# Holding back the odd mixer's first weight splits, and moving the even mixer's first scores by one and two products

## The chip, the cores and the metric

The kernel runs on one core of a Trainium2 chip. The metric is the device time of one execution in microseconds. The engines are TensorE (PE: matmuls, and PEld: its weight loads), VectorE (DVE), ScalarE (ACT), GpSimd (POOL) and SyncE (SP, which here only issues transfers). Each engine works through its own queue in order.

## The reference, cut to what matters

A trunk of two layers over 256 tokens of width 1024, in float32:

```
for layer in (0, 1):
    x = x + 0.5 * swiglu(rms_norm(x), gate, up, down)     # 2816 hidden columns
    x = x + mixer(rms_norm(x))                            # even mixer in layer 0, odd mixer in layer 1
    x = x + 0.5 * swiglu(rms_norm(x), gate, up, down)
return rms_norm(x)
```

The even mixer has two groups of eight heads: "a" is global attention with normed queries and keys and a 2-D rotary, "b" is windowed attention with a 1-D rotary and a sink. The odd mixer is neighbourhood attention with a learned bias table, 16 heads. Each mixer ends with an output projection.

## The kernel before

The stages are numbered 0 to 5: SwiGLU (0), even mixer (1), SwiGLU (2), SwiGLU (3), odd mixer (4), SwiGLU (5). The tokens are two tiles of 128 (`tt` is 0 or 1).

**Products and splits.** Each float32 product is made of three matmuls of rounded parts: high by high, high by low, low by high. `mm` issues these three (lines L471 to L473) and then calls `tick`. Weights come by DMA into tiles called `raw` (three of them, plus a smaller kind). They are then split: ScalarE copies the high part (`hi`, L479), VectorE subtracts to get the low part (`lo`, L482). A split of the mixers is "narrow": it is made in two halves of 128x512, each called a split below, and each half serves one product per token tile. The SwiGLUs' weights are split in double width, 128x1024. The tiles for finished parts are limited: `FIT["wp"]` is 7, each holding two halves, and one is free again when both of its halves were used by both token tiles. When the last split of a `raw` tile is made, the next `raw` transfer is issued on SP's queue.

**The order of the work.** Nothing is planned on the chip: the order in each engine's queue is the order in which the Python code issues the instructions, and that is set by `tick`. Each product makes one tick. In a tick first the pending low part is issued, then every task that is due takes a step (a task is a generator that yields the number of ticks until its next step), and then the supply of splits is advanced:

```
            self.due += self.rate
            n = self.whole[0].step() if self.whole else 1
            if self.due >= n and self.room():
                self.due = min(self.due - n, n)
                self.supply()
```

So `rate` is the number of splits per product. If a product's split has not been made when the product is issued, `mm` makes it at once. Where code must wait for a task's result (`ready`, `finish`, the loop in `out_proj`), it calls `tick(False)`: tasks step, but no product is issued and no split is supplied.

**The end of a SwiGLU.** The down projection runs over 11 pairs of hidden blocks in the order of `DOWN`; some are done by Strassen's seven products (`seven`), whose accumulators "1", "5", "6" and "7" are added to x by the task `combine` (a step per product, eight steps) when the last Strassen pair is through. Then `ENDS` sets the rate and sets `due` to 0. The last two pairs (`HELD`) follow as 16 products, ordered by token tile and half of the columns, so that after each four products `add_to_x` (L614) can add one quarter of x. Five ticks after that, `prepare` transposes the quarter on TensorE (L527) for the next stage.

**The odd mixer.** Two groups of eight heads; for each, keys, queries and values are projected in turn: six projections of 16 products, each using eight new splits in the first eight products (token tile 0) and the same eight again (token tile 1). `natural` turns keys and queries over on TensorE (L549), and ScalarE and VectorE split them (`okTz`, `okTx`, `oqT`). `ODD_RATE` has the rate of each projection and of the two parts of the output projection. The attention runs as a task beside the products.

**The even mixer.** One projection for the keys and values of both groups, then queries of "b", queries of "a", and the output projection for "b" and for "a", 16 products each. `queries` waits `ROPE_WAIT` ticks for VectorE's rotary before the transposes of the queries of "b" (L549). `attend` starts one pair of heads after the other, `EVEN_GAP` ticks apart; each pair issues scores (L1055, L1056, L1059), maxima, exponentials (L1095), normalising (GpSimd, L1109), transposes (L1117) and products with the values (L1040). Group "b" is done before group "a" begins. The output projection of "a" needs its results `oTa00h` and so on, and waits for them with `tick(False)`.

Of the kernel before, what the change touches and what calls it, by code (L numbers as in the profile page):

```python
# [57 lines left out]
SUMS_WAIT = [8, 2]  # L58
SILU_WAIT = [3, 4, 2]
NAT_WAIT = 2  # L60
ROPE_WAIT = [3, 3]
KB_WAIT = {
    "a": [8, 7],
    "b": [8, 9],
# [68 lines left out]
class Split:  # L133
# [3 lines left out]
    def __init__(self, raw, uses, last=False, narrow=False, kind="wp", then=None):  # L137
        self.raw, self.last, self.narrow, self.kind, self.then = raw, last, narrow, kind, then
        n = raw.shape[1]
        self.left = sum(uses[i % len(uses)] for i in range(n))  # L140
        self.parts, self.made = None, 0
# [64 lines left out]
class Trunk:  # L206
# [4 lines left out]
    def __init__(self, ctx, tc, a, out):  # L211
        self.ctx, self.tc, self.nc, self.a, self.out = ctx, tc, tc.nc, a, out
        pool = lambda name, bufs, **kw: ctx.enter_context(tc.tile_pool(name=name, bufs=bufs, **kw))
        self.one = pool("one", 1)
        self.ph = None
        self.raw = pool("raw", RAWS)
        self.wp = pool("wp", FIT["wp"])

        self.two = pool("two", 2)
        self.acc = pool("acc", 1, space=PSUM)  # L220
        self.n = 0
        self.rate = RATE[0]
        self.tasks, self.last, self.last_v = [], [], [[], []]
        self.units, self.whole, self.queue, self.due, self.half = self.plan(), [], [], 0, None
        self.live = {kind: 0 for kind in FIT}
        self.ahead = len(FIRST) - RAWS

        self.hts = {}

    def name(self, s):  # L230
# [56 lines left out]
    def room(self):  # L287

        if not self.whole:
            return False  # L290
        split = self.whole[0]
        return split.made > 0 or self.live[split.kind] < FIT[split.kind]


# [364 lines left out]
    def ffn(self):  # L659
# [197 lines left out]
        for ci, w in enumerate(FF_CHUNKS):  # L857
# [11 lines left out]
            for tt in range(NT):  # L869
                g = both[tt] if self.now.n + ci == 0 else self.project(self.ready(tt), G, tags[tt])  # L870
# [9 lines left out]
        for tt in range(NT):  # L880
            both = self.project(self.now.hT[tt], V, "s")
            s = self.t([P, 512], "silu", SILUS[self.now.n])
# [25 lines left out]
        def seven(pair, first, last):  # L908
            b11, b21, b22, t7, t5, t8, t6 = self.take(7)
            if first:  # L910
                for task in tasks:
                    self.finish(task)
                self.rate = DOWN_RATE[self.now.n]
            f = 2 * pair
            while f not in sums:
                self.tick(False)

            def temp(name, tag, lh, piece):
                if first:
                    M[name] = self.bank(tag)  # L920
                self.mm(M[name], lh, piece, first, last)

            d3, d1, d2, d4 = sums[f]
            temp("1", "pj", gT[0][f + 1], b11)
            self.mm(Y[0][0], gT[0][f], b21, False, False)
            self.mm(Y[0][1], d4, b22, False, False)
            temp("7", "tp", d3, t7)
            temp("5", "s", d1, t5)
            self.mm(Y[1][0], gT[1][f], t8, False, False)
            temp("6", "tp", d2, t6)  # L930

        def combine():

            op = nc.vector.scalar_tensor_tensor
            x = lambda tt, i: self.x[tt][:, i * 512 : i * 512 + 512]
            more = lambda o, y: nc.vector.tensor_tensor(o, o, y, op=ALU.add)
            c = self.t([P, 512], "silu", SILUS[self.now.n])
            nc.scalar.activation(c, M["1"], AF.Copy, scale=0.5)
            op(x(0, 0), M["1"], 0.5, x(0, 0), op0=ALU.mult, op1=ALU.add)
            yield 1  # L940
            v = self.t([P, 512], "silu", SILUS[self.now.n])
            op(v, M["6"], 0.5, c, op0=ALU.mult, op1=ALU.add)
            yield 1
            w = self.t([P, 512], "glu", 3)
            op(w, M["7"], -0.5, v, op0=ALU.mult, op1=ALU.add)
            yield 1
            y = self.t([P, 512], "silu", SILUS[self.now.n])
            op(y, M["5"], 0.5, v, op0=ALU.mult, op1=ALU.subtract)
            yield 1
            more(x(0, 1), y)  # L950
            z = self.t([P, 512], "glu", 3)
            yield 1
            op(z, M["5"], 0.5, w, op0=ALU.mult, op1=ALU.subtract)
            yield 1
            more(x(1, 0), w)
            yield 1
            more(x(1, 1), z)

        order = [i for i, (kind, _) in enumerate(down) if kind == "strassen"]
        for i, (kind, pair) in enumerate(down[:-HELD]):  # L960
            if kind == "strassen":
                seven(pair, i == order[0], i == order[-1])
                if i == order[-1]:
                    self.start(combine())
                    self.rate, self.due = ENDS[self.now.n]
                continue
            for f in (2 * pair, 2 * pair + 1):
                W[f] = self.take(2)
                for tt in range(NT):
                    for half in range(2):  # L970
                        use(f, tt, slice(half * 512, half * 512 + 512))
# [12 lines left out]
                self.start(self.add_to_x(tt, sl, Y[tt][sl.start // 512] if to is None else to, 0.5))  # L984


    def attend(self, qT, has_q, kT, v, has_v, tag, dest, gap, waits, norm, sink=None, bias=None, scale=None):

        nc = self.nc
        pT, sums, exs = {}, {}, {}

        def pair(tt, b0, s):
            wait = iter(waits[tt * 4 + b0 + s])
            if s == 0:
                sums[tt, b0] = self.little([P, 2, 2], "sums", 4)
                exs[tt, b0] = None if sink is None else self.little([P, 2, 2], "es", 4)
            e = exs[tt, b0]
            S = self.scores(tt, b0, s, qT(tt), kT, sink is not None)  # L1000
            yield next(wait)
            src, m, by = self.maxima(S, tt, b0, s, sink, bias, scale)
            if e is not None:
                nc.gpsimd.tensor_tensor(e[:, s, :], sink[:, s * 4 + b0 : s * 4 + b0 + 2], m, op=ALU.add)
            yield next(wait)
            p = self.exps(src, m, by, sums[tt, b0][:, s, :])
            if e is not None:
                nc.scalar.activation(e[:, s, :], e[:, s, :], AF.Exp)
            self.normalise(p, sums[tt, b0][:, s, :], None if e is None else e[:, s, :], norm)
            yield next(wait)  # L1010
            tb = self.transposed(p)
            yield next(wait)
            pT[tt, b0, s] = self.t([P, 2, 2, P], "pt", 4)
            flat = pT[tt, b0, s].rearrange("p a b c -> p (a b c)")
            nc.scalar.activation(flat, tb, AF.Copy)
            if s == 0:
                return
            yield next(wait)
            O = self.bank("o")[:, : 2 * P]
            while not has_v():  # L1020
                yield 1
            self.weigh(O, b0, v, pT[tt, b0, 0], pT[tt, b0, 1])
            yield next(wait)
            yield from self.split_psum(O, 2, f"{tag}{tt}{b0}", dest[tt])

        for tt in range(NT):
            for b0 in (0, 2):
                for s in range(2):
                    while not has_q(tt, b0):
                        yield 1  # L1030
                    self.start(pair(tt, b0, s))
                    yield gap[tt * 4 + b0 + s]
        while len(dest[NT - 1]) < 4:
            yield 1
# [125 lines left out]
    def even(self, sink):  # L1160
# [8 lines left out]
        kT = {g: self.keys_tiles([P, T], f"kT{g}") for g in "ab"}  # L1169
        vv = {g: [self.t([P, P], f"v{g}{tt}") for tt in range(NT)] for g in "ab"}  # L1170
        qT = {g: [[], []] for g in "ab"}
# [26 lines left out]
        def queries(g, tt, ps):  # L1198
# [12 lines left out]
            else:  # L1211
                self.rope(nc.vector, qr, x, 8, axial[g], *tab[g][tt][:2], r)
                yield ROPE_WAIT[tt]
            tb = self.turned(qr.rearrange("p j s d -> p (j s d)"))
# [3 lines left out]
        def heads(g):  # L1218
            return self.attend(
                lambda tt: qT[g][tt],  # L1220
                lambda tt, b0: len(made[g]) > 2 + tt and all(task[1] is None for task in made[g][: 3 + tt]),
                lambda b: kT[g],
                lambda b, s, kc: vv[g][kc][:, s * HD : s * HD + HD],
                lambda: True,
                f"oT{g}",
                oT[g],
                EVEN_GAP[g],
                EVEN_WAITS[g],
                nc.gpsimd,
                sink=sink if g == "b" else None,  # L1230
                scale=(lambda tt, b, s: by[tt][:, s * 4 + b : s * 4 + b + 2]) if g == "a" else None,
            )
# [333 lines left out]
```

## Time and profile before

| what | value |
|---|---|
| median of 3 runs | 942.59 us (941.84 to 943.52) |
| the profiled execution | 942.41 us, span 940.6 us |
| TensorE busy | 921.9 us (98%) |
| VectorE busy | 782.9 us (83%) |
| ScalarE busy | 677.8 us (72%) |
| GpSimd busy | 92.5 us (10%) |

The span is the time from the first to the last instruction of the program; the rest of the execution's time lies around it. A row of the timeline has the start in us, the duration in us, the engine, the line of the kernel, the operation, output and inputs by the kernel's names, the shape, and the count of like instructions merged into the row. A bracket at the end gives how long the engine sat idle before the row, and what released it. Several matmuls overlap in TensorE's pipeline, so the time from one start to the next is what a matmul costs there, not its duration.

### The profile page before, as it was taken

What the parts mean: (1) busy time and instruction counts of PE and PEld (TensorE: products, weight loads), DVE (VectorE), ACT (ScalarE), POOL (GpSimd) and SP (SyncE); (2) the same over time, 40 slices, a digit from 0 to 9 for tenths busy, and PEclk for the clock granted to TensorE, in tenths of its full rate; (3) what the DMA queues carried; (4) which work ended last, traced back from release to release, by engine and by line L of the source; (5) the groups of instructions that cost most, each with busy time, mean ns of one, the idle gap of its engine ahead of it and who ended that gap; (6) DMA issues with size and microseconds to landing.
All of it is one profiled execution on the core that took longest, in us unless ns stands there. A gap on an engine that the chain in (4) does not pass through costs nothing.

```text
span 940.6 us, 12391 instructions
## 1 busy us (share of the span) xinstructions
PE 921.9 (98%) x4399; PEld 752.7 (80%) x4399; DVE 782.9 (83%) x1212; ACT 677.8 (72%) x1091; POOL 92.5 (10%) x152
## 2 busy tenths in 40 slices
PE   9999999999999999999999999999999999999997
PEld 6887888877878788888888878778878788878886
DVE  6799778778869989888978897999767687986997
ACT  7678975477787778875657778657877577768753
POOL 1300000064410000000100000008030000000001
PEclk9999999999999999999999999999999999999999
DMA  8857875554326577766467777565534458487761
GB/s 297 282 166 247 250 234 194 182 152 106 101 91 201 205 231 233 236 212 250 152 179 228 194 239 224 210 244 172 164 106 136 134 178 247 139 253 217 230 224 45
DMA packets 129343, 183.16 MB, mean 195 GB/s; under 512 B 50688, under 2 KB 63744, under 8 KB 129280
## 3 DMA queue, kind: packets, MB, share of 16 engines
q1 hardware_dynamic: 128704, 181.58, 60.9%
q8 instruction: 34, 0.56, 0.2%
q10 hardware_dynamic: 576, 0.79, 0.2%
q14 instruction: 29, 0.24, 0.1%
HBM read 169.76 MB, written 1.05 MB: 182 GB/s over the span
## 4 chain that ended last, share of the span: by engine, by line
PE 66%; DVE 16%; ACT 10%; DMA 4%; issue 3%; POOL 0%; SPq 0%; POOLq 0%; ACTq 0%; DVEq 0%
PE pj L471 9%; PE pj L472 9%; PE pj L473 9%; PE s L472 9%; PE s L473 9%; PE s L471 9%; DVE lo L482 7%; ACT hi L479 3%; DMA glu<-turned 2%; ACT turned L560 2%; DVE raw L395 2%; PE o L1040 2%; ACT shi L479 2%; PE tp L1117 1%; PE o L473 1%
## 5 line engine op out<-in xcount | busy, mean ns | idle before, releaser
L482 DVE TENSOR_TENSOR lo<-raw,hi 128x1024 fp32r<-128x1024 f32 (+1 forms) x372 | 375.9, 1030 | 80.8 <-ACT hi L479 79.3
L479 ACT ACTIVATE hi<-raw 128x1024 fp32r<-128x1024 f32 (+1 forms) x372 | 318.4, 889 | 49.9 <-PE pj L473 12.2
L471 PE MATMUL pj<-hi,th 128*128 128x512 f32 x367 | 146.7, 400 | 0.9 <-ACT glu L766 0.9
L472 PE MATMUL s<-lo,th 128*128 128x512 f32 x373 | 145.5, 390 | 0.9 <-DVE lo L482 0.7
L471 PE MATMUL s<-hi,th 128*128 128x512 f32 x373 | 146.2, 392 | 0.0
L472 PE MATMUL pj<-lo,th 128*128 128x512 f32 x367 | 143.9, 392 | 2.3 <-DVE lo L482 2.0
L473 PE MATMUL s<-hi,tl 128*128 128x512 f32 x373 | 145.3, 390 | 0.0
L473 PE MATMUL pj<-hi,tl 128*128 128x512 f32 x367 | 143.3, 390 | 0.0
L472 PEld LDWEIGHTS pj<-lo,th 128*128 128x128 f32 x367 | 69.1, 188 | 17.6 <-DVE lo L482 5.1
L472 PEld LDWEIGHTS s<-lo,th 128*128 128x128 f32 x373 | 70.0, 188 | 16.2 <-DVE lo L482 2.0
L473 PEld LDWEIGHTS s<-hi,tl 128*128 128x128 f32 x373 | 70.0, 188 | 14.6
L471 PEld LDWEIGHTS s<-hi,th 128*128 128x128 f32 x373 | 70.0, 188 | 14.3
L471 PEld LDWEIGHTS pj<-hi,th 128*128 128x128 f32 x367 | 69.0, 188 | 15.4 <-ACT glu L766 1.3
L473 PEld LDWEIGHTS pj<-hi,tl 128*128 128x128 f32 x367 | 68.9, 188 | 14.6
L491 POOL TENSOR_TENSOR rstd<-var,mhalf 128x1 f32<-128x1 f32 (+2 forms) x16 | 17.1, 1069 | 594.3 <-ACT th L512 315.3
L560 ACT COPY turned<-glu 128x1024 uint16<-128x1024 uint16 (+1 forms) x48 | 60.1, 1252 | 10.3 <-DMA glu<-turned 10.3
L556 ACT COPY turned<-glu 128x1024 uint16<-128x1024 uint16 (+1 forms) x48 | 46.3, 965 | 23.8 <-DVE glu L794 17.5
L479 ACT ACTIVATE shi<-raw 128x1024 fp32r<-128x1024 f32 x30 | 31.8, 1058 | 42.0 <-DVE raw L395 26.1
L471 PE MATMUL s<-hi,g_h 128*128 128x512 f32 (+1 forms) x131 | 51.3, 392 | 0.0
L473 PE MATMUL s<-hi,g_l 128*128 128x512 f32 (+1 forms) x131 | 50.9, 388 | 0.0
L472 PE MATMUL s<-lo,g_h 128*128 128x512 f32 (+1 forms) x131 | 50.8, 388 | 0.0
L482 DVE TENSOR_TENSOR slo<-raw,shi 128x1024 fp32r<-128x1024 f32 x30 | 36.7, 1222 | 9.9 <-ACT shi L479 9.5
(482 smaller groups left out, 1672.4 us busy)
## 6 DMA issues: line engine op xcount, KB each, us to landing
raw<-in_ffn_w_down SPq DMA_DIRECT2D x44, 1024.0 KB, 5.1
raw<-in_ffn_w_up SPq DMA_DIRECT2D x28, 1024.0 KB, 5.1
raw<-in_ffn_w_gate SPq DMA_DIRECT2D x26, 1024.0 KB, 5.2
raw<-in_ffn_w_gate SPq DMA_DIRECT2D x35, 512.0 KB, 3.9
raw<-in_ffn_w_up SPq DMA_DIRECT2D x32, 512.0 KB, 4.9
raw<-in_odd_w_qkv SPq DMA_DIRECT2D x12, 1024.0 KB, 5.8
raw<-in_even_w_in SPq DMA_DIRECT2D x4, 1024.0 KB, 5.0
raw<-in_even_w_out SPq DMA_DIRECT2D x8, 512.0 KB, 5.9
```

The costliest lines, as they stand in the source:

```text
L395: add = lambda o, x, y: self.nc.vector.tensor_tensor(o, x, y, op=ALU.add)
L471: mm(ps, h, wh, start=first, stop=False)
L472: mm(ps, h, wl, start=False, stop=False)
L473: mm(ps, l, wh, start=False, stop=last)
L479: self.nc.scalar.activation(hi, src, AF.Copy)
L482: self.nc.vector.tensor_tensor(lo, src, hi.bitcast(F32), op=ALU.subtract)
L491: nc.gpsimd.tensor_tensor(r[:, :n], v[:, :n], self.mhalf[:, :n], op=ALU.pow)
L556: self.nc.scalar.copy(planes.rearrange("p (h c) -> p h c", h=2), back.rearrange("p (c h) -> p h c", h=2))
L560: self.nc.scalar.copy(planes.rearrange("p (c h) -> p h c", h=2), back.rearrange("p (h c) -> p h c", h=2))
L1040: self.nc.tensor.matmul(O[64 * s : 64 * s + 64, i * P : i * P + P], v(b0 + i, s, kc), pT[s][:, i, kc, :], start=(kc == 0), stop=(kc == 1),)
L1117: nc.tensor.transpose(tb[:, o : o + P], p[:, i, kc * P : kc * P + P], self.ident)
```

## The change

Three things. The class gets a flag `held_back`; while it is set, `room` refuses narrow splits. It is set when the down projection of stage 3 begins and cleared in the last step of `combine`. `ROPE_WAIT` for token tile 0 goes from 3 to 4 ticks. `attend` gets a parameter `late`: the number of ticks that a token tile's first scores are put off after its queries are there; group "b" of the even mixer passes `LATE` (1 for tile 0, 2 for tile 1).

```diff
-ROPE_WAIT = [3, 3]
+ROPE_WAIT = [4, 3]
+LATE = [1, 2]
...
+        self.held_back = False
...
         split = self.whole[0]
+        if self.held_back and split.narrow:
+            return False
         return split.made > 0 or self.live[split.kind] < FIT[split.kind]
...
             more(x(1, 1), z)
+            self.held_back = False
 
         order = [i for i, (kind, _) in enumerate(down) if kind == "strassen"]
+        self.held_back = self.now.n == 3
...
-    def attend(self, qT, has_q, kT, v, has_v, tag, dest, gap, waits, norm, sink=None, bias=None, scale=None):
+    def attend(self, qT, has_q, kT, v, has_v, tag, dest, gap, waits, norm, late=(0, 0), sink=None, bias=None, scale=None):
...
                     while not has_q(tt, b0):
                         yield 1
+                    if b0 + s == 0 and late[tt]:
+                        yield late[tt]
                     self.start(pair(tt, b0, s))
...
                 nc.gpsimd,
+                late=LATE if g == "b" else (0, 0),
                 sink=sink if g == "b" else None,
```

## The prediction

> **What bounds the kernel now.** I read the page first, then TensorE's gaps in the timeline, then the vector and scalar queues at those gaps, then the rows of the odd mixer.
>
> ```profile
> span 940.6 us, 12391 instructions
> PE 921.9 (98%) x4399; PEld 752.7 (80%) x4399; DVE 782.9 (83%) x1212; ACT 677.8 (72%) x1091; POOL 92.5 (10%) x152
> PEclk9999999999999999999999999999999999999999
> raw<-in_odd_w_qkv SPq DMA_DIRECT2D x12, 1024.0 KB, 5.8
> ```
>
> TensorE is busy for 98% of the span at full clock, so a change pays only where it closes a gap of TensorE, and costs where it opens one. Here are the four gaps that the change aims at: three in the even mixer, one at the end of the third SwiGLU.
>
> ```profile
> 208.10 0.30 PE L549 MATMUL tp<-mats,qr 128*128 128x128 f32 x1 [0.65 <-DVE kTax L482]
> 210.80 0.38 PE L1055 MATMUL s<-kTbz,qTb 128*128 128x256 f32 x1 [0.58 <-DVE qTb L482]
> 222.01 0.36 PE L1055 MATMUL s<-kTbz,qTb 128*128 128x256 f32 x1 [0.97 <-ACT p L1095]
> ...
> 632.89 0.33 PE L527 MATMUL tp<-mats,x 128*128 128x128 f32 x1 [2.06 <-DVE x L614]
> ```
>
> The number in brackets is TensorE's idle time before the row. They sum to 0.65 + 0.58 + 0.97 + 2.06 = 4.26 us, which is the most that the change can gain, 0.45% of the span. Why the fourth is there:
>
> ```profile
> 623.65 0.39 PE L473 MATMUL tp<-shi,k12l 128*128 128x512 f32 x1
> ...
> 623.91 2.50 DVE L482 TENSOR_TENSOR lo<-raw,hi 128x512 fp32r<-128x512 f32 x4 [1.35 <-ACT hi L479]
> 627.10 1.29 DVE L482 TENSOR_TENSOR lo<-raw,hi 128x512 fp32r<-128x512 f32 x2 [0.70 <-ACT hi L479]
> 628.32 0.68 DVE L939 SCALAR_TENSOR_TENSOR x<-pj,x 128x512 f32<-128x512 f32 x1
> ...
> 632.16 0.68 DVE L614 SCALAR_TENSOR_TENSOR x<-o,x 128x512 f32<-128x512 f32 x1
> ```
>
> The last Strassen product ends at 624.04, but VectorE first works off six narrow splits of odd weights (4 + 2) and waits for their transfers, so `combine` starts at 628.32 and the x that the transposes need is there only at 632.84.
>
> **The hold: what it gains.** With the six splits gone from VectorE's queue, `combine`'s first operation needs only the accumulator "1", and the second the accumulator "6" at 624.04. Six operations of 0.68 take it to about 628, before the transposes' turn at 632.89 - 2.06 = 630.83. The gap closes: 2.06 gained, and some 0.1 of issue behind it; I take 2.2.
>
> **The hold: what it costs.** Nothing is removed; the six splits come later, so the odd mixer starts with fewer in hand. Counting by `tick`: in before, six are made by the start of the 16 held products, and room (seven tiles, four of them held for down) then refuses more until the 13th; 7, 8 and 9 come at products 13, 14 and 16. In the changed kernel `combine` releases at product 7 with due = 7 x 0.34 = 2.38, so splits come at 7, 8, 10, 13 and 16: five in hand instead of nine. From there the rates and nearly the same remainder (0.06 against 0.02) apply, so each place in the scalar and vector queues at which before makes split n + 4 makes split n in the changed kernel. So the cost is read from before's own rows: when is the low part of n + 4 done, and when does TensorE need the low part of n (its L472 matmul)? First and second projection, splits 8, 15 and 16:
>
> ```profile
> 640.59 3.75 POOL L1301 TENSOR_TENSOR bias<-rows,mats 128x384 f32<-128x384 f32 x3
> 644.46 0.68 DVE L482 TENSOR_TENSOR lo<-raw,hi 128x512 fp32r<-128x512 f32 x1
> 643.90 0.40 PE L472 MATMUL pj<-lo,th 128*128 128x512 f32 x1
> ...
> 654.23 1.39 DVE L482 TENSOR_TENSOR okTx<-tp,okTz 64x512 fp32r<-64x512 f32 x2 [0.23 <-ACT okTz L479]
> 655.65 1.07 DVE L482 TENSOR_TENSOR lo<-raw,hi 128x512 fp32r<-128x512 f32 x1
> 656.64 1.42 DVE L482 TENSOR_TENSOR lo<-raw,hi 128x512 fp32r<-128x512 f32 x1
> 655.08 0.39 PE L472 MATMUL pj<-lo,th 128*128 128x512 f32 x1
> 655.76 0.39 PE L472 MATMUL pj<-lo,th 128*128 128x512 f32 x1
> ```
>
> Split 8 takes the place of 12: 644.46 + 0.68 = 645.14 against 643.90, 1.2 late. It could be nothing if GpSimd's bias work did not slow VectorE there; bounds 0 and 1.4. Splits 15 and 16 take the places of 19 and 20: 656.72 against 655.08 (1.6 late), 658.06 against 655.76: 2.3 late. These two stand behind the pair of key splits that TensorE's own transposes release, so a delayed TensorE delays them as well. Had they run at the undisturbed 0.68, they would end at 656.30 and 656.98 and still be 1.2 late: bounds 1.2 and 2.5.
>
> The Trainium skill, "SBUF — State Buffer", section "SBUF: two separate sides", says that VectorE and GpSimd share a port pair as an exclusive lock, the loser being blocked for the whole instruction. The rows show splits stretched to 1.07 and 1.42, so contention is there; if a split had to sit out a whole bias instruction (estimate from the row above: 3.75 / 3 = 1.25), the first projection's term would be 1.2 + 1.25 = 2.5 instead of 1.2, while the measured stretch is at most 0.74.
>
> Third, fifth and sixth projection:
>
> ```profile
> 667.47 1.28 ACT L1095 ACT_TABLE_LOAD   x1
> 669.76 0.61 ACT L479 ACTIVATE hi<-raw 128x512 fp32r<-128x512 f32 x1
> ...
> 668.24 0.69 DVE L482 TENSOR_TENSOR lo<-raw,hi 128x512 fp32r<-128x512 f32 x1
> 670.62 0.69 DVE L482 TENSOR_TENSOR lo<-raw,hi 128x512 fp32r<-128x512 f32 x1
> 667.01 0.39 PE L472 MATMUL pj<-lo,th 128*128 128x512 f32 x1
> 667.70 0.39 PE L472 MATMUL pj<-lo,th 128*128 128x512 f32 x1
> ...
> 701.88 1.38 DVE L482 TENSOR_TENSOR okTx<-tp,okTz 64x512 fp32r<-64x512 f32 x2
> 703.30 1.30 DVE L482 TENSOR_TENSOR lo<-raw,hi 128x512 fp32r<-128x512 f32 x2
> 700.96 0.40 PE L472 MATMUL pj<-lo,th 128*128 128x512 f32 x1
> ...
> 716.69 0.68 DVE L482 TENSOR_TENSOR lo<-raw,hi 128x512 fp32r<-128x512 f32 x1
> 715.88 0.40 PE L472 MATMUL pj<-lo,th 128*128 128x512 f32 x1
> ```
>
> Third: split 22 takes the place of 26, done at 668.93 against 667.01: 1.9 late. By the count 23 is not made at all when its product comes, and `mm` forces it, behind the table load and the first exponentials; the next place there is 669.76 on ScalarE and 670.62 on VectorE, done 671.31 against 667.70: 3.6 late. Bounds 1.9 and 3.8; I take 3.6, since the exponentials are issued one product ahead of it. The forced split is not charged to `due`, so from here the deficit is three. Fourth: with three the places suffice (split 32 takes that of 35, long in time): nothing, at most 0.5. Fifth: split 39 takes 42's place, the first of the pair at 703.30, done 703.99 against 700.96: 3.0 late, again behind key splits that TensorE releases; bounds 2.4 (without VectorE's slowed work beside GpSimd) and 3.3. Sixth: split 47 takes 50's place, done 717.37 against 715.88: 1.5; bounds 0.8 and 1.8. There 48 is forced (deficit two), in the out projection 54; their low parts miss by some 0.2 (bounds 0 and 0.6).
>
> Fourth SwiGLU: its double-width splits come two products later. The fourth would then stand behind this quartet:
>
> ```profile
> 759.59 1.21 DVE L482 TENSOR_TENSOR lo<-raw,hi 128x1024 fp32r<-128x1024 f32 x1
> 761.31 1.12 DVE L517 SCALAR_TENSOR_TENSOR tl<-tp,mats,th 128x128 fp32r<-128x128 f32 x4 [0.51 <-ACT th L512]
> 761.99 0.39 PE L472 MATMUL s<-lo,th 128*128 128x512 f32 x1
> ```
>
> It ends at 761.31 + 1.12 + 1.21 = 763.64 against 761.99: at most 1.7, at least 0; I take 0.9. After that the tiles' limit brings both kernels together. On SP's queue the odd transfers start about four splits later behind the same tiles; they land in 5.8 us, three tiles lie ahead, and the row-bias loads on SP wait for GpSimd alone: nothing, or at the dearest a fraction of one landing, already inside the upper bounds.
>
> Sum of stalls: 1.2 + 2.3 + 3.6 + 0 + 3.0 + 1.5 + 0.2 + 0.9 = 12.7; by the low ends 0 + 1.2 + 1.9 + 2.4 + 0.8 = 6.3, by the high ends 1.4 + 2.5 + 3.8 + 0.5 + 3.3 + 1.8 + 0.6 + 1.7 = 15.6.
>
> **The even mixer's delays.** ROPE_WAIT puts one product ahead of the query transposes. Two successive products are 667.70 - 667.01 = 0.69 apart, enough for the 0.65. LATE with it puts the first half's scores two products later (0.58 is covered by 1.4) and the second half's four (0.97 by 2.7). Gained: 2.20. But the second group of heads starts only when the first is done, so four products later too, and the out projection waits for it without products in between:
>
> ```profile
> 245.45 0.28 PE L1055 MATMUL s<-kTaz,qTa 128*128 128x256 f32 x1
> 250.28 0.57 ACT L1095 ACTIVATE p<-s,m,by 128x256 f32<-128x256 f32 x1
> 254.73 0.44 PE L1117 MATMUL tp<-mats,p 128*128 128x128 f32 x2 [0.16 <-POOL p L1109]
> 258.96 0.48 PE L471 MATMUL pj<-hi,oTa00h 128*128 128x512 f32 x1
> ```
>
> From that group's first scores (245.45) to the product that needs them (258.96) TensorE now has eight products to run; four of them would already be done. The wait at 254.73 shows it is already close to the limit. Up to 4 x 0.69 = 2.7 comes back as waits; nothing comes back if ScalarE and VectorE, which reach the first exponential 4.8 us after the scores, catch up. Halfway: 1.3. GpSimd's normalising moves with its pair. Net gain 0.9, bounds -0.5 and 2.2.
>
> **Total.** 12.7 - 2.2 - 0.9 = +9.6 us. The profiled execution took 942.41 us (span 940.6 and 1.8 around it), 0.2 under the median of 942.59; from the median, 952.2 us.
>
> **Rivals.** (1) Faster: scalar and vector engines run ahead. Both are idle more in the changed kernel around 624 to 628, and ScalarE's splits wait for no product; if the places of splits 12, 19 and 20 move earlier by 2.3 us relative to TensorE, no low part of the first two projections is late, and later ones little: -2.2 - 2.2 = -4.4, 938.2 us. It decides if the low part for product 16 is done before 655.76 on before's clock. Against: those splits stand behind key splits that a TensorE transpose releases. (2) The stalls do not add: one wait makes TensorE late once, and later splits, which do not wait for TensorE, are then in time. The cost is the largest, 3.6, against 3.1 gained: +0.5, 943.1 us, no measurable change. For it: ScalarE is only 72% busy. Against: the same key and query splits in each projection. (3) The hold does nothing because room already refuses: excluded by the six splits at 623.91 and 627.10.
> (4) TensorE slows after a long wait: a wait of 3.6 in one piece, and the next 3.4 us of products at half clock, cost about 1.7 more each time; at the third projection and once more, 952.2 + 3.4 = 955.6 us. Against: after the 2.06 gap the clock row shows full speed, and by my rows the 3.6 comes in two pieces. The Trainium skill, "TensorE: Matmul & The Clock Gate", "Part 1: The HAM clock gate", halves the clock after an idle window of about 3.4 us; the trace has no gap that long.
>
> **How the numbers follow.** Forecast 0.70, (1) 0.13, (2) 0.12, (4) 0.05. A change of 0.2% (1.9 us) is about what a measurement of this kernel can tell from none. Case (2) lies within it, mostly: of its 0.12, 0.06 is the same, 0.06 slower. With (4) and the forecast, slower is 0.81, the same 0.06, faster 0.13. The forecast's own bounds: 6.3 - 4.4 = +1.9 to 15.6 - 1.7 = +13.9, so 944.5 to 956.5. The range takes in (2) and (4): 943 to 957, leaving out (1) and a little at either end.
>
> **What would show it.** The 2.06 gap at the third SwiGLU's end gone, `combine` straight behind its last product; the even gaps of 0.65, 0.58 and 0.97 gone, and new waits before the product on oTa00h. In the odd mixer TensorE waiting for `lo` of L482 at the eighth product of the first projection, the seventh and eighth of the second and third, the seventh of the fifth and sixth, 1 to 4 us each. I am wrong if these waits are under 1 us, or if only one of them appears.

## The result, and the profile after

The changed kernel takes 968.56 us (median of 4 runs, 966.93 to 969.33); before took 943.06 beside it (4 runs, 941.84 to 944.61). The ratio is 1.0267 [1.0245, 1.0289]: slower by 25 us, where 9.6 were forecast. The profiled execution took 967.88 us.

The head of the page of the changed kernel:

```profile
span 966.1 us, 12376 instructions
PE 932.6 (97%) x4399; PEld 756.0 (78%) x4399; DVE 783.9 (81%) x1212; ACT 677.3 (70%) x1091; POOL 89.9 (9%) x152
```

The same 4399 matmuls, but TensorE is busy for 932.6 us instead of 921.9: no work was added, so some of it ran slower or overlapped less. Half clock (below) accounts for some 5 of these 10.7 us. The rest lies mostly where new waits are: in the first odd projection, at full clock, busy time grew by 0.7 us beside two of them. What is left of the 25.5 us is idle time. For the table below the same products were matched in the two traces, and the growth of the shift of their starts was taken over each stretch (us; negative is gained). "Hold alone" and "filled" are experiments a1 and d1 below.

| stretch | forecast | after | hold alone | filled |
|---|---|---|---|---|
| even mixer, up to the queries of "a" | -1.23 | -0.73 | 0 | 0 |
| queries of "a" | -0.97 | +1.15 | 0 | 0 |
| output projection of "b" | +1.3 | +6.67 | 0 | 0 |
| end of third SwiGLU (held products) | -2.2 | -2.23 | -2.24 | -2.24 |
| odd projection 1 | +1.2 | +2.32 | +2.29 | +2.33 |
| odd projection 2 | +2.3 | +3.83 | +2.27 | +2.26 |
| odd projection 3 | +3.6 | +5.37 | +5.35 | +3.78 |
| odd projection 4 | 0 | +0.01 | +0.01 | +0.01 |
| odd projection 5 | +3.0 | +4.61 | +4.83 | +3.24 |
| odd projection 6 | +1.5 | +1.71 | +1.66 | +1.67 |
| output projection | +0.2 | +0.45 | +0.50 | +0.46 |
| fourth SwiGLU, first 16 products | +0.9 | +2.23 | +2.30 | +2.24 |
| shift at the end | +9.6 | +25.5 | +17.2 | +14.35 |

(A column's sum can miss its last line by some tenths, since the start of the span differs a little from execution to execution.)

The hold did what it was meant to do. Vector queue and TensorE at the third SwiGLU's end, changed kernel:

```profile
629.65 0.68 DVE L943 SCALAR_TENSOR_TENSOR x<-pj,x 128x512 f32<-128x512 f32 x1
...
634.49 0.68 DVE L618 SCALAR_TENSOR_TENSOR x<-o,x 128x512 f32<-128x512 f32 x1
636.29 1.29 DVE L486 TENSOR_TENSOR lo<-raw,hi 128x512 fp32r<-128x512 f32 x2
637.84 0.60 PE L531 MATMUL tp<-mats,x 128*128 128x128 f32 x4
```

`combine`'s first operation no longer has the six narrow splits ahead of it, the splits (L486, before L482) come after it, and the transposes' row has no bracket: the 2.06 gap is gone. Then TensorE in the first three odd projections and the fifth, and one low part of the first:

```profile
648.52 0.50 PE L476 MATMUL pj<-lo,th 128*128 128x512 f32 x1 [1.35 <-DVE lo L486]
650.15 0.50 PE L476 MATMUL pj<-lo,th 128*128 128x512 f32 x1 [0.23 <-DVE lo L486]
663.78 0.50 PE L476 MATMUL pj<-lo,th 128*128 128x512 f32 x1 [1.13 <-DVE lo L486]
665.12 0.55 PE L476 MATMUL pj<-lo,th 128*128 128x512 f32 x1 [0.38 <-DVE lo L486]
678.58 0.50 PE L475 MATMUL pj<-hi,th 128*128 128x512 f32 x1 [0.55 <-ACT hi L483]
680.07 0.50 PE L476 MATMUL pj<-lo,th 128*128 128x512 f32 x1 [0.99 <-DVE lo L486]
681.50 0.50 PE L475 MATMUL pj<-hi,th 128*128 128x512 f32 x1 [0.70 <-ACT hi L483]
682.44 0.76 PE L476 MATMUL pj<-lo,th 128*128 128x512 f32 x1 [0.43 <-DVE lo L486]
720.49 0.80 PE L476 MATMUL pj<-lo,th 128*128 128x512 f32 x1 [2.52 <-DVE lo L486]
645.10 3.36 DVE L486 TENSOR_TENSOR lo<-raw,hi 128x512 fp32r<-128x512 f32 x1
```

Most of these are the waits for `lo` (L476, before L472) that the prediction named. In the second, fifth and sixth projection they stand at the products it named. In the third they stand at the sixth and seventh product instead of the seventh and eighth (splits 22 and 23 are the sixth and seventh), and the high part is waited for as well (L475). In the first the sixth and seventh product wait, and the eighth doesn't. Behind the waits of three projections the granted clock falls. Windows of the changed kernel (columns: busy us and count of PE, PEld, DVE, ACT, POOL, then the granted clock, the DMA share, GB/s):

```profile
658.00:665.40 7.40, 5.89 (x26) 4.16 (x25) 6.17 (x9) 3.35 (x6) 4.81 (x6) 1.00 0.62 174
665.40:668.90 3.50, 3.50 (x10) 2.72 (x10) 0.69 (x1) 1.20 (x2) 1.07 (x2) 0.51 0.79 240
682.50:686.00 3.50, 3.50 (x11) 2.95 (x12) 0.48 (x1) 0.20 (x1) 0.00 (x0) 0.51 0.48 139
720.00:723.50 3.50, 3.01 (x10) 2.42 (x10) 1.46 (x3) 0.41 (x1) 0.00 (x0) 0.51 0.28 93
```

Before the program's last few us, the clock's records give three stretches at half clock, from 665.44, 682.50 and 720.05, each 3.413 us long. A stretch loses half of itself, 1.7 us, so 5.1 of the 25.5 us are clock. Without it projections 2, 3 and 5 cost about 2.1, 3.7 and 2.9 (an estimate; a1 and d1 below have 2.3, 3.8 and 3.2 there at full clock).

### The profile page after: what moved, and what is told of

It is laid out like the page before. It is cut to its first block, busy times and chain, and to the rows that moved or that the text cites. A ratio compares the mean times of both kernels' runs of the same rounds, so it can differ in the third digit from the quotient of the medians.

```text
span 966.1 us, 12376 instructions
## 1 busy us (share of the span) xinstructions
PE 932.6 (97%) x4399; PEld 756.0 (78%) x4399; DVE 783.9 (81%) x1212; ACT 677.3 (70%) x1091; POOL 89.9 (9%) x152
## 5 line engine op out<-in xcount | busy, mean ns | idle before, releaser
L486 DVE TENSOR_TENSOR lo<-raw,hi 128x1024 fp32r<-128x1024 f32 (+1 forms) x372 | 377.0, 1033 | 100.6 <-ACT hi L483 99.0
L476 PE MATMUL pj<-lo,th 128*128 128x512 f32 x367 | 146.5, 399 | 10.2 <-DVE lo L486 9.9
L475 PE MATMUL pj<-hi,th 128*128 128x512 f32 x367 | 148.4, 404 | 2.8 <-ACT hi L483 2.0
L476 PE MATMUL s<-lo,th 128*128 128x512 f32 x373 | 145.7, 391 | 2.4 <-DVE lo L486 2.4
L475 PE MATMUL s<-hi,th 128*128 128x512 f32 x373 | 146.2, 392 | 0.0
L476 PEld LDWEIGHTS pj<-lo,th 128*128 128x128 f32 x367 | 70.1, 191 | 28.7 <-DVE lo L486 16.1
L475 PEld LDWEIGHTS pj<-hi,th 128*128 128x128 f32 x367 | 69.9, 190 | 19.0 <-ACT hi L483 3.6
L476 PEld LDWEIGHTS s<-lo,th 128*128 128x128 f32 x373 | 70.0, 188 | 18.3 <-DVE lo L486 4.2
L475 PEld LDWEIGHTS s<-hi,th 128*128 128x128 f32 x373 | 70.0, 188 | 14.5 <-ACT hi L483 0.3
L475 PE MATMUL s<-hi,g_h 128*128 128x512 f32 (+1 forms) x131 | 51.3, 392 | 0.0
L476 PE MATMUL s<-lo,g_h 128*128 128x512 f32 (+1 forms) x131 | 50.8, 388 | 0.0
L486 DVE TENSOR_TENSOR slo<-raw,shi 128x1024 fp32r<-128x1024 f32 x30 | 36.7, 1222 | 10.7 <-ACT shi L483 10.3
```

The source lines that it names most:

```text
L475: mm(ps, h, wh, start=first, stop=False)
L476: mm(ps, h, wl, start=False, stop=False)
L486: self.nc.vector.tensor_tensor(lo, src, hi.bitcast(F32), op=ALU.subtract)
```

## The experiments

**Which part costs what.** First each part alone: a1 keeps the hold, a2 the even mixer's two edits.

```diff
# a1_hold_only
-ROPE_WAIT = [4, 3]
-LATE = [1, 2]
+ROPE_WAIT = [3, 3]
+LATE = [0, 0]
# a2_even_only
-        self.held_back = self.now.n == 3
```

> The hold alone, the even mixer as before. Theory 'lead' (five splits in hand instead of nine at the start of the odd mixer): the odd mixer's losses of the changed kernel stay whole (+20.5 from odd start to the middle of the fourth SwiGLU, three half-clock stretches of 3.4 us among them) and the gap at the third SwiGLU's end goes (-2.2): +18.3, so 961 us. Rival 'even mixer upsets what follows': clearly less, under 955 us.

> ROPE_WAIT and LATE alone, no hold. If the two parts are independent: +7.2 as in the changed kernel between the even mixer's keys and its second output projection, so 950 us, and nothing after it. Rival 'the even part was predicted rightly and the loss is only a timing accident of the changed kernel': -1 to -2, 941 to 942 us.

a1 took 959.66 us against 944.56, 1.0166 [1.0151, 1.0182]; a2 951.93, 1.0081 [1.0066, 1.0096]. Both parts lose. By the traces the hold's 17.2 and the even mixer's 7.1 make up nearly the whole; the changed kernel has one half-clock stretch more than a1, behind projection 2. a2 came out 2 above its expected 950: in its trace half clock follows the 2.06 gap at the third SwiGLU's end, which the edit doesn't touch, and 1.94 are lost there.

**Is it the hold, or the lead of splits?** c4 has no hold and none of the even edits: five splits are made early, where before makes them, and no more until the odd mixer begins with the `due` of the changed kernel. a3 and a4 keep the hold alone, but raise the rate when `combine` releases it, so that more than five splits are in hand at the odd mixer's start.

```diff
# c4_lead5_no_hold, against before
+        if self.now.n == 3:
+            self.allowed = 5          # room() counts narrow splits down from it
...
+        self.allowed, self.due = None, 0.06
# a3_hold_lead9, against a1 (a4_hold_lead7: 0.61 for 0.8)
-            self.held_back = False
+            if self.held_back:
+                self.held_back, self.rate = False, 0.8
```

> No hold: splits are made ahead of combine as in before, but only five, and none more until the odd mixer starts with due 0.06. Theory 'lead': the same waits in the odd mixer as with the hold (+2.3, 2.3 to 3.8, 5.4, 0, 4.6, 1.7, 0.4, 0.1, 2.3 by projection) though combine still stands behind five splits (gap 1.4 to 2.1): 961 to 965 us. Rival 'holding itself harms': 946 us or less.

> The hold, but when combine ends the supply rate is 0.8 instead of 0.34 for the nine products left, so by the count nine splits are in hand at the start of the odd mixer, as in before. Theory 'lead': the odd mixer runs as in before and only the gap of 2.06 goes: 941 us, no half-clock stretch. Rival 'the later transfers of odd weights or the order of combine cost the time': 955 us or more. Rival 'catching up': nine splits within nine products crowd the low parts of hT: a gap of 1 to 3 us at the end of the third SwiGLU or in the first projection, 942 to 944 us.

> The same with a rate of 0.61: seven splits in hand. Theory 'lead': between the two. By before's rows with each split two places later, the waits left are those of split 24 (third projection) and 40 and 48, some 1 us each, and no half clock: 943 to 946 us. Rival 'lead is not the cause': 955 or more, like a1.

c4 took 960.9 us against 943.81, 1.0187 [1.0171, 1.0203]. Without any hold it shows the same losses: 3.83, 5.35, 4.76 and 1.70 in projections 2, 3, 5 and 6, and 2.29 in the fourth SwiGLU. There the short lead costs, not the holding. The first projection differs: c4 was expected to lose 2.3 there and loses 0.37, with the same lead; why is shown by d2 below. a3 took 941.56 (8 runs) against 944.56, 0.9974 [0.9964, 0.9985]: **faster than both kernels.** Its page and its release:

```profile
span 939.7 us, 12392 instructions
PE 921.9 (98%) x4399; PEld 752.4 (80%) x4399; DVE 783.9 (83%) x1212; ACT 677.5 (72%) x1091; POOL 93.0 (10%) x152
630.88 0.60 PE L531 MATMUL tp<-mats,x 128*128 128x128 f32 x4
```

The gap is gone here too (no bracket), 2.24 gained; the first projection loses 0.22, and nothing else changes. (The medians differ by 3.0. Half clock behind the gap in some of before's runs would explain it, but those runs weren't traced.) a4 took 944.59, 1.0004 [0.9994, 1.0013], the time expected, but not by the waits expected: the first four projections are covered, and the lead gives out later, with waits like this one in the fourth SwiGLU, which loses 2.35 in all:

```profile
762.09 0.50 PE L476 MATMUL s<-lo,th 128*128 128x512 f32 x1 [1.15 <-DVE lo L486]
```

**Does the half clock cost by itself?** c3 and d1 add to a1 small matmuls by a tile of zeros in the waits (35 in each trace, where the expectation below says 31), so that TensorE stays busy without being any earlier. In c3 some stood at the wrong products; d1 places them by the trace.

```diff
# c3_hold_filled, against a1
+        ahead, between = self.fills.pop(id(piece), (0, 0))
+        for _ in range(ahead):
+            mm(ps[:HD], self.zlhs, self.prev, start=False, stop=False)
         mm(ps, h, wh, start=first, stop=False)
+        for _ in range(between):
+            mm(ps[:HD], self.zlhs, wh, start=False, stop=False)
# d1_hold_filled2, against c3
+FILLS = {(0, 1): {5: (0, 5)}, (0, 0): {6: (0, 4), 7: (0, 1)}, (0, 2): {5: (2, 4), 6: (3, 1)}, (1, 0): {3: (1, 0), 6: (0, 10)}, (1, 2): {6: (1, 3)}}
```

> The hold alone, and in its waits of the odd mixer 31 matmuls by zeros (0.23 us each, added to the same accumulator), put just where TensorE would wait for a split. Theory 'clock': the half-clock stretches of a1 (two of 3.4 us, 1.7 us lost in each) come from TensorE standing still, so with the matmuls there are none and 959.7 becomes 956 to 957 us. Rival 'the clock drops for another reason' or matmuls by zeros do not count: two or more stretches, 959.5 us or more.

> As c3, with the matmuls by zeros put where the profile of the hold alone has its waits: sixth product of the first projection, seventh and eighth of the second, sixth and seventh of the third, fourth and seventh of the fifth, seventh of the sixth. Theory 'clock': no half clock in the odd mixer, and the matmuls now hide in the waits: 16.6 to 17.2 of shift in the odd mixer become 13 to 14, 956 to 957 us against 959.7 of the hold alone. Rival 'the clock costs nothing on its own' (what TensorE loses at half clock it would lose waiting for later splits anyway): 959 to 960 us.

c3 took 960.51 us against 943.81, 1.0179 [1.0164, 1.0194]: no half clock in the odd mixer, but misplaced fills cost as much as that saved (projection 1 lost 2.77). d1 took 956.95 against 943.5, 1.0141 [1.0126, 1.0156]. The same 3.41 us after the third projection's waits, in a1 (first row) and in d1:

```profile
674.70:678.11 3.41, 3.41 (x11) 2.73 (x10) 0.23 (x1) 1.46 (x3) 0.00 (x0) 0.51 0.70 213
```

```profile
674.70:678.11 3.41, 3.41 (x19) 2.88 (x18) 0.77 (x2) 1.85 (x4) 0.00 (x0) 1.00 0.57 165
```

Eleven matmuls at half clock against 19 at full clock in the same time. The table's last two columns differ in projections 3 and 5 alone: by 1.57 and 1.59. So a stretch costs 1.6 to 1.7, over and above the wait. (By the medians d1's gain over a1 is smaller than the traces' 2.9: 13.5 over its before against 15.1, where the runs of before on a1's chip themselves spread from 942.59 to 945.56.)

**What sets off the half clock?** Not the length of a gap: the pair of 1.13 and 0.38 in projection 2 is followed by half clock in the changed kernel, and the same pair in a1 is not. In each profile, though, all half-clock stretches begin a whole number of 3.413 us apart (665.44, 682.50 and 720.05 are 5 and 11 such steps), while the remainder differs from execution to execution. So three kernels were run once more unchanged, for another place of these windows against the same gaps.

> The kernel before, unchanged, once more. Theory (fixed windows): the clock is decided at the ends of windows of 3.413 us that run on regardless of the program; TensorE's idle time inside one window counts, not the length of a gap. In the profiles so far every window with 1.8 us or more of idle time was followed by one at half clock, none with under 1.3, and between them both happen. Then every half-clock stretch of this execution starts a whole number of 3.413 us from the others, and one follows the 2.06 gap at the third SwiGLU's end if that gap lies in one window with 1.8 us or more, and none if the border cuts it so that less than 1.3 lies in each; time 942 to 943 without, about 944.5 with. Rival (the gap alone decides): no half clock inside the program, as in the profile of before, and 942.4 within 0.5.

> The changed kernel, unchanged, once more. Fixed windows: the gaps of the odd mixer are the same as in the first profile (1.35, 1.13 and 0.38, the four of the third projection, 2.52), but the windows lie elsewhere against them, so the pair of 1.13 and 0.38 is followed by half clock only if one window holds 1.3 us or more of it; the 2.52 gap of the fifth is nearly always followed by one. Starts a whole number of 3.413 us apart. 1.7 us more or less for each stretch more or less than three. Rival (the gaps alone decide): the same three stretches behind the same products, and 967.9 within 0.5.

> The hold alone, unchanged, once more. Fixed windows: its gaps are those of the odd mixer of the changed kernel; in its first profile the border lay between the gaps of 1.14 and 0.37 of the second projection (no half clock there), and stretches followed the third and the fifth. This time the starts have another remainder against 3.413 us, and which of the three projections drop follows from the idle time in each window (1.8 and more always, under 1.3 never). Rival (the gaps alone decide): the same two stretches and 959.6 within 0.5.

The three settle that the gaps alone don't decide. The window that ends with projection 2's waits, and the one behind it, in a1 and then in e3, from their own windows:

```profile
654.27:657.68 3.41, 2.27 (x9) 1.22 (x7) 3.10 (x4) 1.39 (x3) 3.21 (x5) 1.00 0.78 295
657.68:661.09 3.41, 3.04 (x15) 2.38 (x15) 1.16 (x2) 1.21 (x2) 1.87 (x2) 1.00 0.50 126
```

```profile
655.87:659.28 3.41, 1.88 (x8) 1.18 (x8) 2.50 (x3) 0.08 (x2) 3.30 (x4) 1.00 0.41 157
659.28:662.69 3.41, 3.41 (x10) 2.57 (x9) 0.69 (x1) 1.20 (x2) 0.57 (x1) 0.50 0.91 287
```

In a1 the border falls between the two gaps (1.14 before it, 0.37 behind it) and the clock stays at 1.00. In e3 both lie in one window, 1.53 us idle, and the next runs at 0.50. e3 took 961.31 us, 1.67 above a1's 959.64, with three stretches instead of two. e2 took 969.89 against 967.88: four windows at half clock, among them one behind the even mixer's 2.30 gap, which the first profile had left at full clock; this time projection 2's pair had 1.38 in one window, and no half clock followed. So e2 and e3 both refute the rival, though 1.53 and 1.38 lie where the theory foretold neither outcome. e1 took 943.61: no half clock inside the program, with 1.27 and 0.83 of the gap's 2.11 in two windows, as the windows say; but it spent 1.2 more between the even mixer and the third SwiGLU's end, which no theory here had foreseen, so its time tells nothing apart. Over all 19 profiles, 24 half-clock stretches inside the programs began behind windows with 1.36 to 2.81 us idle; all 16 windows with 1.84 or more were followed by one; the idlest without had 1.76. Of the fifteen windows from 1.36 up to 1.76 seven were followed by half clock (e3's 1.53 was, one of 1.53 in e1 was not); what decides there stays open.

The Trainium skill, "TensorE: Matmul & The Clock Gate", "Part 1: The HAM clock gate", says that the window is 3413 ns long and free-running; these traces agree (3.413 us, a new remainder in each execution). It also says that the clock halves after an idle window; here a window in which TensorE was busy for more than half was enough (1.88 of 3.41 us in e3).

**Why did the first projection lose 2.3 and not 1.2?** In a1 the low part that it waits for, GpSimd's work, and the product:

```profile
638.20 3.37 DVE L486 TENSOR_TENSOR lo<-raw,hi 128x512 fp32r<-128x512 f32 x1
638.29 2.73 POOL L1310 TENSOR_TENSOR bias<-rows,mats 128x384 f32<-128x384 f32 x3
641.62 0.51 PE L476 MATMUL pj<-lo,th 128*128 128x512 f32 x1 [1.36 <-DVE lo L486]
```

d2 starts that bias work five products later:

```diff
# d2_hold_bias_later, against a1
-BIAS_WAIT, BIAS_GAP = 4, [0, 3]
+BIAS_WAIT, BIAS_GAP = 9, [0, 3]
```

> The hold alone, with BIAS_WAIT 9 instead of 4, which puts GpSimd's first bias work behind the second token tile's rstd in its queue. Theory 'shared port': the sixth split's low part, 3.37 us long where three bias operations ran beside it, takes 0.7 again, and the first projection loses 0 to 0.5 instead of 2.3; the later projections keep their waits: 957 to 958.5 us. Rival 'place in the queue' (the split is late for its place behind hT's low parts, not for GpSimd): first projection still 1.2 to 2.3, 959.7 us.

```profile
640.02 0.69 DVE L486 TENSOR_TENSOR lo<-raw,hi 128x512 fp32r<-128x512 f32 x1
...
654.63 2.59 DVE L486 TENSOR_TENSOR lo<-raw,hi 128x512 fp32r<-128x512 f32 x2
```

The low part is back at 0.69, and the first projection loses 0.36 instead of 2.29: shown, and c4's 0.37 agrees, where that low part took no more than 1.27. But the bias work now lies beside the second projection's splits (two of them 2.59), whose waits grow from 1.5 to 2.5. The total, 961.04 against 943.5, 1.0185 [1.0168, 1.0202], misses the expected time. In the trace four windows run at half clock instead of a1's two, some 3.4 us, while the rest is some 1.9 less than in a1: the collision's cost went in part, and the clock took more than was saved.

**Why did the even mixer lose 7 us?** Each of its edits alone, then a2 with group "a" let go when two of the second half's pairs of "b" are done instead of four, and two kernels that also put off the queries of "a":

```diff
# b1_rope_only, against a2:   LATE = [0, 0]
# b2_late_first, against a2:  ROPE_WAIT = [3, 3], LATE = [1, 0]
# b3_late_second, against a2: ROPE_WAIT = [3, 3], LATE = [0, 2]
# b4_even_a_early, against a2
-        while len(dest[NT - 1]) < 4:
+        while len(dest[NT - 1]) < (2 if late[1] else 4):
# c1_rope_qa, against b1:     QA_WAIT = [10, 10]  (was [9, 9])
# c2_even_qa, against a2:     QA_WAIT = [13, 13]
```

> ROPE_WAIT [4, 3] alone, no LATE, no hold. Theory 'place in the queue': the transposes lose their 0.65 wait, but one more weight split now stands ahead of the query's low parts on VectorE, so the first scores come no earlier than 212.3 and wait some 1.7 instead of 0.58; all later pairs are one product later. Sum at the start of group a's queries +0.6; at the second output projection +1 to +2: 945.5 to 946.5 us. Rival 'as predicted': the 0.65 goes and nothing else: 944 us.

> LATE [1, 0] alone: every pair of group b one product later, the query transposes where they were. Theory 'each product by which the pairs slip behind the projections costs cover at the end': the wait of 0.58 goes, up to a quarter of the changed kernel's 6.7 between the first and second output projection comes: +1, 945.5 us. Rival 'collision': the slip puts pairs beside other work of group a's queries, and the cost is not in proportion: 947 us or more, or a gain.

> LATE [0, 2] alone: only the second token tile's pairs of group b, two products later, and group a two products later. Theory 'cover': the wait of 0.97 goes, about half of 6.7 comes, +2.4: 947 us. Rival 'as predicted': -0.97 + 0.7: 944 us.

> ROPE_WAIT and LATE as in the changed kernel, no hold, but group a begins when the first two of group b's four results of token tile 1 are there, so it is about as early as in before. Theory 'cover': the 3.8 that the wait for oTa00h grew by (6.2 to 9.9 us from the last product on oTb12h to the first on oTa00h) goes; the 3 us lost earlier, beside group a's queries, stay: 948 us. Rival 'collision alone': more pairs at once make the earlier part worse, 952 us or more.

> ROPE_WAIT [4, 3] alone, and QA_WAIT 10 instead of 9 for both token tiles, so that group a's query norms keep their distance to group b's pairs. Theory 'GpSimd's order' (with ROPE_WAIT alone the last pair of group b is normalised on GpSimd behind group a's rstd of 1.65 us, which waits for VectorE's sums; TensorE waits 2.78 for it): that wait goes, the stretch from the first to the second output projection grows by at most 2 instead of 6.1, no half clock there: 945 to 947 us. Rival 'cover' (each product of slip costs at the end, whatever GpSimd's order): still 950 us.

> ROPE_WAIT and LATE as in the changed kernel, no hold, QA_WAIT 13 instead of 9. Theory 'GpSimd's order': the wait of 2.30 before the pair's transposes goes, the longer wait for oTa00h (+3.8) stays, the two waits of 1.08 stay: 949 to 950 us against 951.9 without it. Rival 'cover' alone: 952 us.

| run | us | before beside it | ratio | output projection of "b" |
|---|---|---|---|---|
| b1 | 951.64 | 944.16 | 1.0074 [1.0058, 1.0091] | +6.11 |
| b2 | 949.37 | 944.16 | 1.0056 [1.0041, 1.0072] | +5.93 |
| b3 | 947.33 | 944.16 | 1.0039 [1.0025, 1.0053] | +4.41 |
| b4 | 947.73 | 944.16 | 1.0046 [1.0029, 1.0064] | +4.05 |
| c1 | 947.48 | 943.81 | 1.0047 [1.003, 1.0063] | +1.85 |
| c2 | 950.48 | 943.81 | 1.007 [1.0055, 1.0085] | +4.91 |

b1 missed both of its expected times, b2 came out as its rival (947 or more), b3 and b4 near theirs, c1 and c2 half a us above theirs. Part of the times is not the even mixer's: in the traces of b1, b2 and c2, as in a2, half clock follows the gap at the third SwiGLU's end and takes 1.7 to 2.0 there. c1's runs spread from 945.48 to 949.88, and its +1.85 is from a trace at the lower end.

One product of delay (b1, b2) costs nearly as much as all of them together (a2: +6.69), though 1.7 of it is a half-clock stretch that a2 lacks. So it isn't a slope of so much for each product. In b1 a large wait comes at once, and GpSimd's queue shows why. In before:

```profile
237.93 0.93 POOL L1109 TENSOR_SCALAR p<-p,r 128x256 f32<-128x256 f32 x2 [1.80 <-ACT sq L1152]
241.64 1.65 POOL L491 TENSOR_TENSOR rstd<-var,mhalf 128x8 f32<-128x8 f32 x1 [2.78 <-DVE var L489]
```

and in b1, with TensorE behind it:

```profile
242.58 1.65 POOL L495 TENSOR_TENSOR rstd<-var,mhalf 128x8 f32<-128x8 f32 x1 [5.01 <-DVE tot L1111]
244.33 0.28 POOL L1217 TENSOR_SCALAR by<-rstd,rstd 128x8 f32<-128x8 f32 x1
244.58 0.93 POOL L1116 TENSOR_SCALAR p<-p,r 128x256 f32<-128x256 f32 x2
245.11 1.06 PE L1124 MATMUL tp<-mats,p 128*128 128x128 f32 x4 [2.78 <-POOL p L1116]
```

In before the last pair of "b" is normalised ahead of the `rstd` of group "a"'s queries. Delayed by one product it stands behind it in GpSimd's queue, and TensorE's transposes wait 2.78 us. c1 restores the order by putting off the queries of "a" by one product as well:

```profile
242.08 1.45 POOL L1116 TENSOR_SCALAR p<-p,r 128x256 f32<-128x256 f32 x2 [4.67 <-DVE r L1114]
243.50 1.65 POOL L495 TENSOR_TENSOR rstd<-var,mhalf 128x8 f32<-128x8 f32 x1
242.62 0.44 PE L1124 MATMUL tp<-mats,p 128*128 128x128 f32 x2 [0.25 <-POOL p L1116]
```

The gap of 2.78 becomes 0.25 (and 0.53 before the next transposes), the half clock that followed it in b1 (from 245.7) is gone, and the stretch costs 1.85 instead of 6.11.

The changed kernel has a gap of 2.30 at about the same place, but another queue makes it. Before's copy of a pair's transposes, then the changed kernel's rows:

```profile
238.68 0.60 ACT L1015 ACTIVATE pt<-tp 128x512 f32<-128x512 f32 x1
```

```profile
237.88 0.93 POOL L1117 TENSOR_SCALAR p<-p,r 128x256 f32<-128x256 f32 x2 [1.62 <-ACT sq L1160]
239.29 1.20 ACT L483 ACTIVATE qTa<-tp 64x512 fp32r<-64x512 f32 x2 [0.90 <-PE tp L553]
240.51 0.47 ACT L1103 ACTIVATE p<-s,m 128x256 f32<-128x256 f32 x1
242.03 0.59 ACT L1021 ACTIVATE pt<-tp 128x512 f32<-128x512 f32 x1
242.77 0.63 PE L1125 MATMUL tp<-mats,p 128*128 128x128 f32 x4 [2.30 <-ACT pt L1021]
```

GpSimd has normalised this pair by 238.81. Its transposes wait for a `tp` bank, which the copy `pt` of the pair before it frees (there are two such banks, shared with the transposes of the queries). In before that copy stands ahead of the queries of "a" on ScalarE (`qTa`, there at 239.74). Moved later, it stands behind them and behind a third pair's exponentials. c2 puts off the queries of "a" and the gap goes, which fits, but it moves `rstd` and `qTa` alike, so it doesn't tell the two queues apart; the trace does. c2 still loses 4.91 in this stretch. The end of the stretch in the changed kernel:

```profile
258.32 0.38 PE L1063 MATMUL s<-kTaz,qTa 128*128 128x256 f32 x1 [0.81 <-ACT p L1103]
259.79 0.39 PE L1063 MATMUL s<-kTaz,qTa 128*128 128x256 f32 x1 [0.73 <-ACT p L1103]
266.11 0.48 PE L475 MATMUL pj<-hi,oTa00h 128*128 128x512 f32 x1
```

From the start of the last product of "b" to that of the first on `oTa00h` before takes 6.15 us (252.81 to 258.96) and this kernel 9.91 (256.20 to 266.11): 3.8 more. From the first scores of "a" to the same point it is 13.51 (from 245.45) against 12.92 (from 253.19), with four products fewer inside. b4 lets "a" start earlier and gets 2.6 of the 6.7 back, with its time as expected. The remaining shares of this stretch were not separated one by one.

## Why the prediction was right and wrong

**Right: the direction, the hold's gain, and the chain from lead to waits.** The gap closed for 2.23 (2.2). Five splits instead of nine put TensorE at the low parts of projections 2, 3, 5 and 6, at 2.1, 3.7, 2.9 and 1.7 (2.3, 3.6, 3.0, 1.5) and left the fourth alone, as read from before's own rows by shifting splits four places; c4 and a3 show that in these projections the lead alone is the cause. Rival (1), engines that run ahead, and rival (2), stalls that do not add, are refuted by the same rows.

**Wrong: the even mixer (-0.9 forecast, +7.1 measured).** The step that failed is that the pairs of "b" can slip by whole products and cost nothing before the wait for `oTa00h`. The prediction says "GpSimd's normalising moves with its pair" and puts nothing for what a moved pair meets in the other engines' queues. In the changed kernel a pair's copy `pt` falls behind the queries of "a" on ScalarE, 2.30. With one product of delay, in b1, its normalising falls behind `rstd` on GpSimd, 2.78. The one price that was put down, "up to 4 x 0.69 = 2.7 comes back", with 1.3 taken, held as a bound: some 2.2 came back (an estimate: the four products are 2.8, and the path from the first scores of "a" became only 0.6 shorter). The gains were not had either. The 0.65 and 0.58 gave 0.73, since one more weight split now stands ahead of `qTb` on VectorE (three instead of two), and in place of the 0.97 came two new waits:

```profile
212.28 0.36 PE L1063 MATMUL s<-kTbz,qTb 128*128 128x256 f32 x1 [1.08 <-DVE qTb L486]
225.21 0.33 PE L1125 MATMUL tp<-mats,p 128*128 128x128 f32 x1 [1.08 <-POOL p L1117]
228.55 0.33 PE L1125 MATMUL tp<-mats,p 128*128 128x128 f32 x1 [1.09 <-POOL p L1117]
```

The scores still wait for `qTb`: 1.08 instead of 0.58.

**Wrong: the clock (0 forecast, 5.1 measured).** Rival (4) named the mechanism, half clock for 3.4 us at 1.7 each, but got a chance of 0.05, because "by my rows the 3.6 comes in two pieces" and because the 2.06 gap in before left the clock up. Both reasons fall. Pieces add within a window, and where a gap lies against the windows is chance: the same gap at the third SwiGLU's end is followed by half clock in the traces of a2, b1, b2 and c2.

**Wrong place: the first projection (1.2; measured 2.3).** The prediction had the eighth product wait for split 8. In the changed kernel the sixth waits, 1.35, for a low part that met three bias operations in a row and took 3.36 instead of 0.68; the eighth doesn't wait. Without that meeting the same lead costs 0.4 (c4, d2), so the 1.2 stands for a wait that didn't come, and the 2.3 came from another. The estimate of 2.5 by the Trainium skill, "SBUF — State Buffer", section "SBUF: two separate sides", lies near the 2.3 by luck: it is for split 8 and one bias operation, not for three. Blocked, not slowed, fits these rows: 3.37 beside 2.73 in a1, and 0.69 without the overlap in d2.

**Mis-sized: the fourth SwiGLU (0.9, at most 1.7; measured 2.2).** Two splits came late there, not one:

```profile
784.23 0.50 PE L476 MATMUL s<-lo,th 128*128 128x512 f32 x1 [0.68 <-DVE lo L486]
787.36 0.50 PE L476 MATMUL s<-lo,th 128*128 128x512 f32 x1 [0.76 <-DVE lo L486]
```

The misses sum to 8.0 + 5.1 + 1.1 + 1.3 = 15.5 of the 15.9 between +9.6 and +25.5.

## What to carry to other kernels

When supply work is moved out of the way of a late consumer, keep the lead that it had built up: the same hold with the splits caught up at once is the only version that gained. When a step moves by even one product, go through every in-order queue that it issues to, and look at what it now stands behind, not only at what it issues: here it was GpSimd's queue in one version and ScalarE's in the next. Price waits of an otherwise full TensorE by the idle time that falls into one clock window, not by the longest gap.

## What the runs showed of the hardware

Half clock set in after windows of 3.413 us with as little as 1.36 us of idle time, often the sum of several waits, and cost 1.6 to 1.7 us a time; of windows with up to 1.76 some were not followed by it. The place of the windows changes from execution to execution, so that the same kernel with the same waits varied by 1.67 us between two executions (a1 and e3). A low part on VectorE took 3.37 us beside three GpSimd operations that took 2.73 together, and 0.69 away from them.
